# A decoder layer on one core: the down projection of the second feed-forward's last group as seven products of halves, factor columns by VectorE, and a new order

## The chip, the cores and the metric

The kernel runs on one core of one Trainium2 chip. The metric is the device time of one execution in microseconds; the time given for a kernel is the median of its runs. TensorE (PE in the profile; PEld is its loading of weights), VectorE (DVE), ScalarE (ACT), GpSimd (POOL) and the DMA queue of SyncE (SP) work side by side and wait for each other by semaphores. Each engine runs its own instructions strictly in the order in which the program holds them, so an instruction that waits holds up all that stand behind it on its engine.

## The reference

One layer of a decoder with 512 tokens and a width of 1024, all in float32. The two feed-forward parts are the ones that the change touches; `d_ff` is 2816, which is 22 tiles of 128.

```python
x = x + 1/2 * SwiGLU_1(rms(x))
h = rms(x) @ W_in                     # sparse attention (8 heads), stick-breaking attention (8 heads)
x = x + concat_heads(A, B) @ W_out
x = x + CrossAttn(rms(x), rms(mem))   # 4 heads, 256 memory tokens
x = x + 1/2 * SwiGLU_2(rms(x))

def swiglu(h, wg, wu, wd):
    return (jax.nn.silu(h @ wg) * (h @ wu)) @ wd
```

## The kernel before, in words

**Layout.** Everything is held transposed: a tile has 128 features on the partitions and the 512 tokens as columns. The stream `x` is 8 such tiles (`t_81` to `t_88` in the program's names). To keep float32 precision, each operand of a product is split into a high and a low part: ACT rounds it to the high part, DVE subtracts (`wsplit` for weights, `split` for activations). A product of two split operands is three matmuls: high by high, high by low, low by high (`mm3`, or `prod` for the halves).

**Feed-forward.** A tile of the hidden layer needs a gate and an up product over 8 tiles of the input. `ffn_up` does that plainly: 48 matmuls of 512 columns. `wino_up` (line 938) does the two together as a 2 by 2 block product with seven instead of eight products (Winograd's form of Strassen's scheme): the blocks are gate and up weights by the two halves of the inner dimension, times left and right halves of the tokens. Each of its seven products covers 4 tiles of the inner dimension, 256 columns, 3 matmuls: 84 matmuls of 256 columns, or, where the string `WIDE` marks a bank as wide, some of them as one matmul of 512 columns for two. DVE adds weights up before and sums of products behind. `right` makes the sums of the input's blocks.

The down projection is done in three groups of hidden tiles (`GROUPS`; 8, 7 and 7 in the second feed-forward). `ffn_down` (line 995) takes one group and one of the 8 output tiles: it loads the weights, splits them, runs 3 matmuls of 512 columns for each hidden tile of the group into one PSUM bank, and DVE adds the bank to `x` with a factor of -0.5. In the last group this finishes the output tile, which is then stored. The very last output tile is done in two halves of 256 columns in the same bank.

**Banks.** PSUM has 8 banks: 2 with the tag "mm", 5 "at", 1 "sm" (`BANKS`). A bank is taken again only when its last reader is done.

**Factor columns.** `rcol` (line 1135) turns a row factor `r` (the reciprocal root mean square, equal on all partitions, tokens as columns) into a column with the tokens on partitions, times -0.5. It does so with one fp32 matmul of one column for each 128 tokens: `r` as weights, a constant column `one` as operand. It is called once with 4 pieces (for the layer's attention part) and once with 2 (memory).

**Order.** All operations are recorded first, in the order of `FIRST`, `FEED` and `MIDDLE`, strings that list pieces of work (in `FEED`, "5" is the up projection of hidden tile 5, "1.3" the down projection of group 1 for output 3, "ws:0" a weight that is split early and kept in DRAM). The planner (`add_any` at line 271, `attempt` at line 342) then walks through a model of the engines: every operation has a priority, which is its place in the recording with some fixed offsets, and each engine takes the one with the lowest priority among those that are ready and whose tiles fit. All instructions are issued from one line (529 before, 656 in the changed kernel), so the profile names all of them by that line, and tiles by kind: `p` PSUM, `w` split weights or weight sums, `raw` loaded weights, `t` activations, `half` half-width sums, `d` kept weights in DRAM, `cr` and `c` constants, `s` small columns.

**The place in the middle** of which the prediction speaks: `nsa_values` (line 1607) computes the values and gates of the sparse attention for four blocks of tokens, in two "mm" and two "at" banks, 280 columns each. `v_evac` (line 1151) reads 256 of those columns with ACT and DVE, and the remaining 24 go to `gates`. `wout_sb` (line 1623), the first part of the output projection, takes an "mm" bank next. Around the same time `key_rotate` splits the rotated keys, the DVE differences of 64 rows by 512.

## Time and profile before

| | |
|---|---|
| runs, us | 1055.39, 1054.36, 1054.22; median 1054.36 |
| the profiled execution, us | 1056.67 |
| its span, first to last instruction, us | 1054.9 |
| mean granted clock of TensorE | 0.995 |
| instructions | 18656 |
| busy: PE, DVE, ACT, POOL, us | 1043.8, 923.3, 655.5, 50.8 |
| matmuls with weights of `w` or `t` and these on the right: 512 and 256 columns | 2091, 3090 |
| HBM read, written, MB | 136.93, 22.02 |

Rows of groups have the count of instructions, the busy time, the mean of one, and the idle time of the engine in front of them with what ended it. Rows of the timeline have the start, the length, the engine, the operation, the tiles and shapes, and in brackets how long the engine stood idle before and what it then followed. A row with x and a number covers so many instructions that follow each other. Busy times of instructions that overlap are counted once.

### The profile page before, as it was taken

How to read it: one execution, taken by the hardware profiler on the slowest of the kernel's cores; microseconds unless marked ns; L12 is line 12 of the kernel's file. 1: busy time of each engine (PE TensorE's matmuls, PEld its weight loads, DVE VectorE, ACT ScalarE, POOL GpSimd, SP SyncE). 2: the span in 40 equal slices, each digit the busy share in tenths (PEclk: the TensorE clock that was granted, in tenths of full speed). 3: DMA queues.
4: the chain of work that ended last, by engine and by line, in shares of the span. 5: the costliest groups of instructions: out<-in, count | busy, mean ns of one | idle time of the engine just before them, and what ended most of it. 6: DMA issues, size and time to landing. Idle time of an engine off the chain costs nothing.

```text
span 1054.9 us, 18656 instructions
## 1 busy us (share of the span) xinstructions
PE 1043.8 (99%) x6391; PEld 932.6 (88%) x6391; DVE 923.3 (88%) x1991; ACT 655.5 (62%) x1396; POOL 50.8 (5%) x93
## 2 busy tenths in 40 slices
PE   9999999999999999999999999999999999999998
PEld 8889999899888889888887888999999999898887
DVE  8999999878778869999899998899999999996842
ACT  7655656545565669899867796887665445442420
POOL 0000000000000000000003342110000000000000
PEclk9999999999999999999989999999999999999999
DMA  8174535767387732622426342654543434443421
GB/s 285 42 260 147 171 105 197 251 212 220 113 282 249 238 120 72 198 101 88 123 83 209 121 143 77 211 180 150 161 131 122 149 121 149 130 138 103 131 89 50
DMA packets 92590, 161.48 MB, mean 153 GB/s; under 512 B 11216, under 2 KB 18000, under 8 KB 92496
## 3 DMA queue, kind: packets, MB, share of 16 engines
q1 hardware_dynamic: 92064, 160.02, 47.3%
q8 instruction: 50, 0.82, 0.3%
q14 instruction: 44, 0.36, 0.1%
q10 hardware_dynamic: 432, 0.29, 0.1%
HBM read 136.93 MB, written 22.02 MB: 151 GB/s over the span
## 4 chain that ended last, share of the span: by engine, by line
PE 86%; DVE 11%; ACT 1%; issue 1%; DMA 1%; SPq 0%; DVEq 0%; ACTq 0%
PE p L529 86%; DVE t L529 7%; DVE w L529 2%; DMA t<-t 1%; ACT t L529 1%; DVE s L529 1%; ACT w L529 0%; DVE raw L529 0%; DVE gates L529 0%; SPq L529 0%; DVEq L529 0%; ACTq L529 0%; DVE one L529 0%
## 5 line engine op out<-in xcount | busy, mean ns | idle before, releaser
L529 PE MATMUL p<-t,w 128*128 128x256 f32 (+1 forms) x5181 | 887.6, 329 | 2.5 <-issue 1.5
L529 PEld LDWEIGHTS p<-t,w 128*128 128x128 f32 x5181 | 765.3, 190 | 90.2 <-DVE t L529 2.7
L529 ACT ACTIVATE w<-raw 128x512 fp32r<-128x512 f32 (+1 forms) x448 | 263.8, 613 | 191.6 <-PE p L529 113.9
L529 DVE TENSOR_TENSOR w<-raw,w 128x512 fp32r<-128x512 f32 (+1 forms) x448 | 293.0, 672 | 59.4 <-PE p L529 26.1
L529 ACT ACTIVATE t<-t 128x512 f32<-128x512 f32 (+9 forms) x463 | 220.2, 510 | 70.4 <-DVE t L529 65.8
L529 DVE TENSOR_TENSOR t<-t,t 128x512 fp32r<-128x512 f32 (+8 forms) x372 | 194.0, 543 | 9.4 <-ACT t L529 7.5
L529 DVE TENSOR_TENSOR t<-p,t 128x256 f32<-128x256 f32 (+4 forms) x194 | 96.4, 516 | 7.8 <-ACT t L529 5.6
L529 DVE SCALAR_TENSOR_TENSOR t<-p,t 128x512 f32<-128x512 f32 (+4 forms) x117 | 73.0, 632 | 30.2 <-PE p L529 28.8
L529 PE MATMUL p<-t,t 128*128 128x256 f32 (+4 forms) x450 | 96.6, 334 | 2.5 <-DVE t L529 1.1
L529 ACT ACTIVATE t<-p 128x256 f32<-128x256 f32 (+5 forms) x157 | 75.9, 502 | 28.1 <-PE p L529 25.8
L529 PEld LDWEIGHTS p<-t,t 128*128 128x128 f32 x450 | 70.7, 191 | 12.1 <-DVE t L529 2.1
L529 PE MATMUL p<-w,t 128*128 128x256 f32 (+2 forms) x304 | 53.4, 334 | 0.5 <-PE p L529 0.5
L529 DVE TENSOR_TENSOR raw<-raw,raw 128x512 f32<-128x512 f32 x76 | 52.2, 687 | 0.6
L529 PEld LDWEIGHTS p<-w,t 128*128 128x128 f32 x304 | 47.7, 202 | 5.2 <-PE p L529 0.9
L529 POOL TENSOR_SCALAR t<-t,s 128x256 f32<-128x256 f32 (+3 forms) x80 | 45.5, 588 | 105.7 <-DVE s L529 78.1
L529 DVE TENSOR_TENSOR t<-p,half 128x256 f32<-128x256 f32 x114 | 44.6, 418 | 2.0 <-PE p L529 1.8
L529 ACT ACTIVATE w<-w 128x512 fp32r<-128x512 f32 x38 | 23.8, 627 | 26.7 <-DVE w L529 21.6
L529 PE MATMUL p<-cr,t 128*128 128x128 f32 (+2 forms) x256 | 39.7, 265 | 0.0
L529 ACT ACTIVATE t<-t,g 128x256 fp32r<-128x256 f32 (+1 forms) x40 | 23.5, 588 | 21.4 <-DVE t L529 19.2
L529 PEld LDWEIGHTS p<-cr,t 128*128 128x128 f32 x256 | 32.0, 152 | 4.2 <-ACT t L529 0.5
L529 PE MATMUL p<-t,cr 128*128 128x512 f32 (+4 forms) x114 | 30.9, 329 | 1.3 <-DVE t L529 1.3
L529 POOL CAST t<-t 64x512 fp32r<-64x512 f32 (+2 forms) x9 | 5.1, 571 | 553.4 <-ACT t L529 471.4
(79 smaller groups left out, 437.9 us busy)
## 6 DMA issues: line engine op xcount, KB each, us to landing
raw<-in_ws_dram SPq DMA_DIRECT2D x362, 256.0 KB, 3.0
w<-d SPq DMA_DIRECT2D x108, 256.0 KB, 3.4
d<-w SPq DMA_DIRECT2D x76, 256.0 KB, 4.2
raw<-in_wraw_dram SPq DMA_DIRECT2D x16, 256.0 KB, 4.0
raw<-in_ws_dram SPq DMA_DIRECT2D x16, 192.0 KB, 2.6
t<-in_xT_dram SPq DMA_DIRECT2D x8, 256.0 KB, 4.4
raw<-in_ws_dram SPq DMA_DIRECT2D x14, 128.0 KB, 3.2
out_dram<-t SPq DMA_DIRECT2D x7, 256.0 KB, 2.0
```

What stands on the lines that cost most here:

```text
L529: return getattr(getattr(self.nc, op.eng), method)(*args, **kw)
```

## The change

It has these parts.

1. The second feed-forward's groups are 7, 7 and 8 hidden tiles. The last group's down projection is done for two output tiles at a time by `seven_down`: a 2 by 2 block product with seven products, of weights (two outputs by two halves of the hidden tiles) and activations (two halves of the hidden tiles by left and right token halves). `mixed` makes the sums of the activations' blocks, for each pair of hidden tiles that stand 4 apart. Of the first four hidden tiles only the left half is split as such. `wino_up` hands back its unsplit result for this.
2. `rcol` multiplies `r` by the identity on DVE and sums over the columns, in one instruction for each 128 tokens, instead of the matmul.
3. Every tile's number, counted as they are made, can have an offset (`SHIFT`), which is added to the priority of the operations recorded while it is the newest. The strings `FIRST`, `WIDE`, `FEED` and `MIDDLE` are new. In `FIRST`, 7 hidden tiles instead of 6 of the first feed-forward are done by `ffn_up`.
4. `ffn_down` takes a bank for each half of its output where it works in halves; that case was the last output of group 2, which `seven_down` now does.

```diff
-FIRST = "a0 up b0 up a2 up b2 a1 b1 a3 up b3 up up"
+FIRST = "a2 up up a0 up a1 up b0 a3 b2 b1 up b3 up up"
-GROUPS = {"1": (6, 8, 8), "2": (8, 7, 7)}
-WIDE = {"1": "z-x-x-xx-xxzxx---xz-xz", "2": "------x-----zz--zzzz--"}
+GROUPS = {"1": (6, 8, 8), "2": (7, 7, 8)}
+SEVEN = {"1": "", "2": "2"}
+WIDE = {"1": "z-z-xzxx-xxxxz-x-xzxzx", "2": "------x-----zz--zzzz--"}
...
+        "2": """0 2 4 5 1 3 6 0.2 0.5 8 0.6 7 13 19 10 0.1 0.0 0.3 12 11 0.7 9 1.3 14 18 1.4 0.4 15 1.0 16 17 1.2 1.5 1.1 20 1.6 21
+1.7 2.2 2.4 2.0 2.6"""}
+SHIFT = """2:-3 3:-3 4:-3 15:-3 16:3 21:120 22:40 24:-150 27:300 36:150 37:150 39:-3 40:-3 41:-3 42:-20 43:-20 44:-20 45:-20
...
-        op.prio = op.idx + self.bias
+        op.seg = self.seg
+        op.prio = op.idx + self.bias + self.shift.get(self.seg, 0)
...
-        self.split(ut, a[0], a[1])
+        c = slice(0, H if half else T)
+        self.split(ut[:, c], a[0][:, c], a[1][:, c])
+        return ut
+    def mixed(self, first, second, u1, u2, D, i):
...
+        minus(t12[:, L], u1[:, L], u1[:, R])
+        negative(t12[:, R], t12[:, L], u2[:, R])
+        minus(t34[:, L], u2[:, R], u1[:, R])
+        negative(t34[:, R], t12[:, R], u2[:, L])
+        D["b11", i] = tuple(x[:, L] for x in first)
+        D["b21", i] = tuple(x[:, L] for x in second)
+        D["b22", i] = tuple(x[:, R] for x in second)
+        for names, t in ((("t1", "t2"), t12), (("t3", "t4"), t34)):
+            parts = self.pair()
+            self.split(t, *parts)
...
+    def seven_down(self, k, c, j, D, done, halves):
...
+        X, Q, V = self.ps("mm")[:, :H], self.ps("at")[:, :H], self.ps("at")
...
+        prod(X, self.wsplit(a11), "b11")
+        nc.scalar.activation(g[:, R], X, AF.Copy)
+        prod(Q, self.wsplit(a12), "b21")
+        nc.vector.tensor_tensor(g[:, L], Q, g[:, R], OP.add)
+        s1 = add(a21, a22, self.wtile("w", F32, NW))
+        prod(V[:, L], self.wsplit(a22), "t4")
+        s3 = add(a11, a21, a21)
+        s2 = add(s1, a11, a11)
+        prod(X, self.wsplit(s2), "t2", first=False)
+        nc.scalar.activation(u2, X, AF.Copy)
+        prod(V[:, R], self.wsplit(s1), "t1")
+        prod(X, self.wsplit(s3), "t3", first=False)
+        nc.scalar.activation(u3, X, AF.Copy)
+        onto(x2, V, 0.5)
+        both = "p (a n) -> p a n"
+        onto(x2.rearrange(both, a=2), u3[:, None, :].to_broadcast([P, 2, H]), 0.5)
+        done(j + 1, slice(0, T))
+        if halves:
+            onto(x1[:, L], g[:, L])
+            done(j, L)
+        s4 = add(a12, s2, a12)
+        prod(V[:, R], self.wsplit(s4), "b22", first=False)
+        if halves:
+            onto(x1[:, R], u2)
+            onto(x1[:, R], V[:, R])
+            done(j, R)
+        else:
+            nc.vector.tensor_tensor(g[:, R], V[:, R], u2, OP.add)
+            onto(x1, g)
+            done(j, slice(0, T))
...
     def rcol(self, r, n):
         nc = self.nc
-        ps = self.ps("sm")
-        for t in range(n):
-            nc.tensor.matmul(ps[:, t:t + 1], r[:, t * P:(t + 1) * P], self.one, start=(t == 0), stop=(t == n - 1),
-                             skip_group_check=True)
         out = self.small([P, NT], tag="rcol", bufs=2)
-        nc.vector.tensor_copy(out[:, :n], ps[:, :n])
+        t = self.t2()
+        for i in range(n):
+            s = slice(i * P, (i + 1) * P)
+            nc.vector.tensor_tensor_reduce(t[:, s], r[:, s], self.cf[:, R_ID:R_ID + P], -0.5, 0.0, OP.mult, OP.add,
+                                           accum_out=out[:, i:i + 1])
         return out
```

In the built program there are now 1980 matmuls of 512 columns and 3276 of 256 of the kind of the table, against 2091 and 3090.

## The prediction

> **What bounds the kernel now.** I read the page's busy table first, then the waits of TensorE, then the time cut into stretches.

> ```profile
> PE 1043.8 (99%) x6391; PEld 932.6 (88%) x6391; DVE 923.3 (88%) x1991; ACT 655.5 (62%) x1396; POOL 50.8 (5%) x93
> ```

> TensorE (PE) is busy for 1043.8 of 1054.9 us. Since overlapping matmuls make that share look better than it is, its waits decide:

> ```profile
> PE p L529 <- DVE t L529: 4.1, 5, 1.3
> PE p L529 <- issue: 1.5, 1, 1.5
> PE p L529 <- DMA t<-t: 1.0, 1, 1.0
> ```

> It waited about 7 us altogether, and the last stretch has next to none of it. The stretches show where VectorE (DVE) has room, in columns of length, busy time of PE, PEld, DVE, ACT and POOL, granted clock and DMA:

> ```profile
> 400.00:500.00 100.00, 100.00 (x572) 87.99 (x572) 93.26 (x213) 92.03 (x203) 2.74 (x4) 1.00 0.37 119
> 530.00:540.00 10.00, 8.28 (x42) 7.67 (x42) 9.94 (x21) 7.93 (x20) 0.00 (x0) 0.66 0.13 38
> 550.00:560.00 10.00, 8.54 (x48) 7.45 (x48) 9.30 (x27) 6.87 (x16) 1.83 (x3) 0.83 0.95 277
> 800.00:900.00 100.00, 100.00 (x703) 93.23 (x702) 99.08 (x193) 50.01 (x86) 0.00 (x0) 1.00 0.45 140
> 900.00:950.00 50.00, 50.00 (x312) 44.80 (x311) 46.12 (x89) 23.32 (x40) 0.00 (x0) 1.00 0.43 131
> 1000.00:1046.00 46.00, 46.00 (x206) 37.96 (x205) 16.99 (x29) 9.27 (x16) 0.00 (x0) 1.00 0.23 75
> ```

> So time follows TensorE's instructions almost everywhere. In 800 to 900 us VectorE is full as well (99.08 of 100) and TensorE still never waits: the two can run level. Only the last 46 us, the down projections that change, leave VectorE 29 us of room. The middle loses both to waits and to a granted clock of 0.66 and 0.83.

> **Price of a matmul.** In the last stage every 21 matmuls of 512 columns end in one read by VectorE:

> ```profile
> 1036.36 0.69 DVE L529 SCALAR_TENSOR_TENSOR t<-p,t 128x512 f32<-128x512 f32 x1 [1.65 <-PE p L529]
> 1041.12 0.69 DVE L529 SCALAR_TENSOR_TENSOR t<-p,t 128x512 f32<-128x512 f32 x1 [4.07 <-PE p L529]
> 1045.88 0.69 DVE L529 SCALAR_TENSOR_TENSOR t<-p,t 128x512 f32<-128x512 f32 x1 [4.07 <-PE p L529]
> ```

> They stand 4.76 us apart: 0.2267 us for a wide matmul. From 200 to 300 us TensorE ran without a gap on two forms:

> ```profile
> L529 PE MATMUL p<-t,w 128*128 128x512 f32 x249 | 61.9, 391 | 0.0
> L529 PE MATMUL p<-t,w 128*128 128x256 f32 x358 | 49.3, 283 | 0.0
> ```

> (100 - 249 x 0.2267) / 358 = 0.1217 us for a narrow one; 800 to 900 us (136 wide, 567 narrow) gives 0.122. I use 0.1218. Two narrow ones thus cost 0.017 more than a wide one: halving products has a price.

> **Down projections.** Group 2 had 8, 7 and 7 tiles: 507 wide and 42 narrow matmuls. Now the first two groups take 336 wide, and the last four pairs 7 products x 4 tiles x 3 = 84 narrow each, 336. That is -171 x 0.2267 + 294 x 0.1218 = -38.77 + 35.81 = -2.96 us.

> **First feed-forward.** A seventh tile is done plainly (48 wide matmuls instead of a seven-product one), and the string of wide banks changes: together +60 wide, -108 narrow = +13.60 - 13.15 = +0.45 us. Both together: **-2.5 us**, all of it on TensorE's path. [...]

> **Factor columns.** Six fp32 products with one column go; each is two passes:

> ```profile
> 368.00 0.95 PE L529 MATMUL p<-one,t 128*128 128x1 f32 x8
> 368.81 1.42 PE L529 MATMUL p<-w,t 128*128 128x512 f32 x5
> 408.15 0.50 PE L529 MATMUL p<-one,t 128*128 128x1 f32 x4
> 408.51 0.36 PE L529 MATMUL p<-t,cr 128*128 128x256 f32 x1
> ```

> From start to the next start: 0.81 + 0.36 = **-1.2 us** of TensorE. VectorE gets six multiply-and-reduce over 128 columns in place of two small copies. Their nearest rows:

> ```profile
> L529 DVE CUSTOM_DVE_ANT_0 t<-p,t 128x512 f32<-128x512 f32 x16 | 10.5, 682 | 0.0
> L529 DVE CUSTOM_DVE_ANT_0 t<-p,t 128x384 f32<-128x384 f32 x16 | 8.5, 549 | 0.3 <-PE p L529 0.3
> L529 DVE DVE_READ_ACCUMULATOR2_ANT s<- 128x1 f32 x32 | 2.6, 82 | 0.0
> ```

> The slope (133 ns per 128 columns) gives 283 + 82 ns, 2.2 us for six. At 400 to 500 us VectorE has 6.7 us free and TensorE does not wait: nothing, or 1.9 us if that room is gone.

> **The end.** The last output was done in two halves of one bank, and the second waited for the read of the first:

> ```profile
> 1048.39 0.42 DVE L529 SCALAR_TENSOR_TENSOR t<-p,t 128x256 f32<-128x256 f32 x1 [1.82 <-PE p L529]
> 1048.87 2.77 PE L529 MATMUL p<-t,w 128*128 128x256 f32 x21 [0.52 <-DVE t L529]
> 1051.67 0.42 DVE L529 SCALAR_TENSOR_TENSOR t<-p,t 128x256 f32<-128x256 f32 x1 [2.86 <-PE p L529]
> ```

> Now the last product adds onto a bank that VectorE reads during the product before it (12 x 0.1218 = 1.46 us against a read of 0.69). The chain behind the last product is the same, one 128x256 read and one store. **-0.5 us** (the bracket of the second row).

> **The middle.** TensorE stood still before the output projection's first product, and the seven matmuls behind ran at 0.41 instead of 0.227 us:

> ```profile
> 555.90 2.87 PE L529 MATMUL p<-t,w 128*128 128x512 f32 x7 [1.46 <-issue]
> 552.26 0.42 DVE L529 TENSOR_SCALAR gates<-p,s 128x24 f32<-128x24 f32 x2
> 553.88 1.39 DVE L529 TENSOR_TENSOR t<-t,t 64x512 fp32r<-64x512 f32 x2
> 555.31 0.88 DVE L529 SCALAR_TENSOR_TENSOR t<-p,s,t 128x256 fp32r<-128x256 f32 x2
> ```

> What it waited for is the "mm" bank, which the read at 555.31 frees. On VectorE, where the combined value projection is read out, stood before (p_1750, p_1751 are its "mm" banks):

> ```order
> L529 TENSOR_SCALAR gates<-p_1750,s_1139 128x24
> L529 TENSOR_SCALAR gates<-p_1751,s_1139 128x24
> L529 TENSOR_TENSOR t_1830<-p_1829,t_1830 128x256
> L529 TENSOR_SCALAR gates<-p_1752,s_1139 128x24
> L529 TENSOR_TENSOR t_1837<-p_1836,c 128x256
> L529 TENSOR_SCALAR gates<-p_1753,s_1139 128x24
> L529 TENSOR_REDUCE s_1831<-t_1830 128x8
> L529 TENSOR_TENSOR t_1744<-t_1688,t_1743 64x512
> L529 TENSOR_TENSOR t_1746<-t_1688,t_1745 64x512
> L529 SCALAR_TENSOR_TENSOR t_1778<-p_1750,s_1139,t_1778 128x4x64
> ```

> and there stands now (p_1748 is the first "mm" bank):

> ```order
> L656 TENSOR_SCALAR gates<-p_1748,s_1174 128x24
> L656 TENSOR_TENSOR t_1969<-p_1968,t_1969 128x256
> L656 TENSOR_SCALAR gates<-p_1749,s_1174 128x24
> L656 TENSOR_REDUCE s_1970<-t_1969 128x8
> L656 TENSOR_SCALAR gates<-p_1750,s_1174 128x24
> L656 SCALAR_TENSOR_TENSOR t_1776<-p_1748,s_1174,t_1776 128x4x64
> L656 TENSOR_TENSOR t_1742<-t_1684,t_1741 64x512
> L656 TENSOR_TENSOR t_1738<-t_1668,t_1737 64x512
> ```

> The read moved ahead of the two 64x512 differences of the rotated keys (1.39 us) and of a gate and an addition. The stall and its slow stretch cost 1.46 + 7 x (0.41 - 0.227) = 2.74 us; between 0 and -2.74 I take **-2.0**, since the read now stands over 1.5 us earlier. [...] The row of 0.83 in this stretch, with no gap beyond 1.46, speaks for the higher figure.

> The other middle stall stays. It waits for the one "sm" bank through a chain of ACT and DVE steps, and the new order has the same products around it, 24 of 64 columns where 27 were:

> ```profile
> 527.61 3.09 PE L529 MATMUL p<-t,t 128*128 128x64 f32 x27
> 531.96 0.76 PE L529 MATMUL p<-t,cr 128*128 128x512 f32 x2 [1.25 <-DVE t L529]
> 533.19 8.02 PE L529 MATMUL p<-w,t 128*128 128x256 f32 x41 [0.47 <-PE p L529]
> ```

> Three fewer at 0.11 us each could lengthen it by 0.3; I count 0.

> **What VectorE gets in the last stage.** Its steps follow each other at 0.60 us for 512 columns, less than the 0.69 shown of one:

> ```profile
> 846.39 0.69 DVE L529 TENSOR_TENSOR raw<-raw,raw 128x512 f32<-128x512 f32 x1
> 846.99 0.69 DVE L529 TENSOR_TENSOR t<-t,t 128x512 fp32r<-128x512 f32 x1
> 847.59 0.69 DVE L529 TENSOR_TENSOR w<-raw,w 128x512 fp32r<-128x512 f32 x1
> 841.18 0.75 DVE L529 TENSOR_TENSOR t<-p,half 128x256 f32<-128x256 f32 x2
> 841.84 0.68 DVE L529 TENSOR_TENSOR w<-w,w 128x512 fp32r<-128x512 f32 x1
> ```

> and 0.33 for 256. A pair of outputs was two times (low part of 512, of 384, one read); it is now, for the second pair of the four (w low part, raw and w weight sums):

> ```order
> L656 TENSOR_TENSOR w_3312<-raw_3301,w_3311 128x512
> L656 TENSOR_TENSOR t_3285<-p_3281,t_3285 128x256
> L656 TENSOR_TENSOR w_3314<-raw_3302,w_3313 128x512
> L656 TENSOR_TENSOR w_3315<-raw_3303,raw_3304 128x512
> L656 TENSOR_TENSOR raw_3303<-raw_3301,raw_3303 128x512
> L656 TENSOR_TENSOR raw_3301<-w_3315,raw_3301 128x512
> L656 TENSOR_TENSOR w_3317<-raw_3304,w_3316 128x512
> L656 TENSOR_TENSOR raw_3302<-raw_3302,raw_3301 128x512
> L656 SCALAR_TENSOR_TENSOR t_84<-p_3282,t_84 128x512
> L656 TENSOR_TENSOR w_3321<-w_3315,w_3320 128x512
> ```

> Sums of one pair now stand between reads of the pair before, so a read that is late holds up the next weights. Per pair: 7 low parts, 4 sums and 3 reads of 512, 2 of 256: 14 x 0.60 + 2 x 0.33 = 9.1 us, against 84 x 0.1218 = 10.2 of TensorE. The operands (four differences of 256, two low parts of 512, less the right half that four tiles no longer split) add 2.5 us for each of four tile pairs before that. Over the whole second feed-forward VectorE has 361 steps of 512, 16 of 384 and 235 of 256 columns (326, 16, 204 before): about 303 us, against 460 wide and 1813 narrow matmuls, 325 us. It fits, as in 800 to 900 us, with little to spare at the end: from the first low part of the first pair on, 62 steps of 512 and 17 of 256, 42.9 us, stand beside 42.3 us of matmuls (336 narrow, 6 wide). TensorE has 73 older matmuls (12.6 us) ahead of that point, VectorE some 5.5 us of steps: a lead of about 7 us. I take **+0.7** for a late weight or two; bounds 0 and, with the 0.69 and 0.42 of single steps and no lead, 49.7 - 42.3 = 7.4. ACT (9 of 46 us there) and DMA (share 0.23, four more stores and loads of kept weights) have room.

> **Sum**, against the profiled execution's 1056.7 us (span 1054.9 and 1.8 around it): -2.5 - 1.2 - 0.5 - 2.0 + 0.7 = -5.5, 1051.2. The median of the runs, 1054.4, lies 2.3 lower: **1048.9 us**.

> **Rivals.**
> - *The middle gives nothing.* TensorE comes earlier to the keys that DMA copies together, where it already waited 1.0 us (the third row of the waits), and waits there instead: 1048.9 + 2.0 = 1050.9. For it speaks that those copies hang on the DMA, against it that two more output products stand before them. 0.18.
> - *The middle gives more*: the slow clock of 0.66 behind 531.96 goes too, at 41 x (0.196 - 0.122) = 3.0 us: 1045.9. The order shows no reason. 0.08.
> - *VectorE late in some pairs*: half of the 7.4 instead of 0.7, 1052. For it: reads stand between the sums. Against it: 800 to 900 us. 0.16.
> - *Slower*: the last stage becomes VectorE's. Each read waits for its product, the sums queue behind, nothing runs ahead: +7.4, and such stalls bring the half clock at 1.3 to 3 us, as at 555.90 and 533.19. 1048.2 + 7.4 + 2 = 1057.6. It decides when the lead at the first pair is gone and steps take over 0.67 us. 0.10.

> The likeliest, as summed, has 0.48; its own range is 1047 to 1050.5.

> **Chances.** 0.2% is about what a measurement here can tell from no change: below 1052.25 is faster, above 1056.47 slower. Faster: 0.48 + 0.17 + 0.08 + 0.04 = 0.77; same 0.13; slower 0.10. The range 1045.5 to 1054.5 leaves out the slower case, the late pairs' upper end and little below.

> **What would show it.** No gap of TensorE over 0.3 us before the output projection's first product near 550 us (the middle), and granted clock above 0.95 there; no product with the column "one"; TensorE without waits in the last 45 us and VectorE above 90% busy; 256-column matmuls at 0.122 each in the last pairs. Waits of TensorE for w behind VectorE in the last four pairs, or a clock below 1 there, would make the prediction wrong.

## The result and the profile after

The changed kernel takes 1045.74 us (median of 1044.51 to 1045.77), the kernel before 1054.88 beside it: a ratio of 0.991, 95% interval 0.9893 to 0.9927, 9.1 us faster. Measured again beside two of the experiments it was 10.3 us faster (0.9903, 0.9887 to 0.992). The forecast was 5.5 us, 1048.9. The direction and most of the places were right, the size was not: 1045.74 lies below the 1047 to 1050.5 of the likeliest case and at the low edge of the whole range, 1045.5 to 1054.5, and the second measurement, 1044.90, lies below that edge. In the table of experiments, one of the five runs of the changed first part took 1444.43 us at a granted clock of 0.655; its ratio leaves that run out.

The profiled execution of the changed kernel took 1045.75 us with a span of 1044.0. First the page's line of the busy times:

```profile
PE 1036.1 (99%) x6454; PEld 931.4 (89%) x6454; DVE 950.1 (91%) x2058; ACT 670.0 (64%) x1424; POOL 49.6 (5%) x92
```

Then the view of TensorE's waits (total us, times, longest):

```profile
PE p L656 <- ACT t L656: 2.2, 4, 1.1
PE p L656 <- DVE t L656: 1.9, 4, 1.1
PE p L656 <- issue: 0.3, 1, 0.3
```

TensorE's waits fell from 7.7 us (6.6 in the three rows shown of before, the rest in smaller ones) to 4.4. VectorE has 27 us more work than before and is still no bound. The stretches, in the columns used before:

```profile
400.00:500.00 100.00, 100.00 (x550) 87.23 (x549) 88.85 (x200) 88.08 (x191) 1.50 (x2) 1.00 0.36 118
530.00:540.00 10.00, 9.48 (x51) 8.48 (x52) 9.86 (x24) 7.80 (x18) 0.00 (x0) 0.69 0.13 40
550.00:560.00 10.00, 9.66 (x60) 8.10 (x58) 9.75 (x28) 6.30 (x17) 1.22 (x2) 1.00 1.01 312
800.00:900.00 100.00, 100.00 (x650) 91.41 (x650) 96.93 (x188) 47.87 (x86) 0.00 (x0) 1.00 0.42 134
1000.00:1044.00 44.00, 40.71 (x337) 40.36 (x335) 34.73 (x62) 17.58 (x35) 0.00 (x0) 1.00 0.26 85
```

At 550 to 560 us the clock is back at 1.00, at 530 to 540 it is about as low as before (0.69 against 0.66). The last stage has TensorE busy to its end (it ends at 1040.7) and VectorE at 34.73 of 44 us. The two places of the middle, from TensorE's timeline:

```profile
530.33 1.30 PE L656 MATMUL p<-t,cr 128*128 128x512 f32 x2 [1.08 <-ACT t L656]
531.82 6.81 PE L656 MATMUL p<-w,t 128*128 128x256 f32 x37 [0.19 <-DVE t L656]
...
552.03 2.29 PE L656 MATMUL p<-t,w 128*128 128x512 f32 x9 [0.34 <-issue]
```

And TensorE's groups by form in the last stage, 1000 to 1044 us (count, busy us, mean ns):

```profile
L656 PE MATMUL p<-t,w 128*128 128x256 f32 x333 | 40.6, 283 | 0.0
L656 PE MATMUL p<-t,w 128*128 128x512 f32 x4 | 1.5, 398 | 0.0
```

The output projection's first product at 552.03 waits 0.34 us where it waited 1.46, and its nine wide matmuls take 2.29 us, at a clock of 1.00. The stall near 530 us is still there, 1.08 and 0.19 us for 1.25 and 0.47. In the last stage no wait is left, and the two last rows with the 40.71 us above give the price of a narrow matmul: (40.71 - 4 x 0.2267) / 333 = 0.1195 us. That is a little low, since the view counts matmuls that began before 1000 us too; from start to start the trace has 0.120 here, as mean and as median, and not 0.1218.

To compare kernels I use one more measure, called loss below: the time from each matmul's start to the next, less the usual start-to-start time of its form (the median over both kernels). It holds waits and half-speed stretches. How a total splits depends somewhat on how finely forms are told apart. Over the whole program the usual times fell by 3.5 us (1018.4 to 1014.9) and the loss by 7.4 (31.9 to 24.5), 5.7 of it ahead of the second feed-forward; with forms told apart by shape alone it is 4.2 and 6.7. The profiled execution of before was one of its longer ones, 1.8 us above its median, so that some 2 us of this is no gain of the change.

### The profile page after: what moved, and what is told of

Read it like the earlier page. It is cut to its first block, busy times and chain, and to the rows that moved or that the text cites. A ratio compares the mean times of both kernels' runs of the same rounds, so it can differ in the third digit from the quotient of the medians.

```text
span 1044.0 us, 18955 instructions
## 1 busy us (share of the span) xinstructions
PE 1036.1 (99%) x6454; PEld 931.4 (89%) x6454; DVE 950.1 (91%) x2058; ACT 670.0 (64%) x1424; POOL 49.6 (5%) x92
## 4 chain that ended last, share of the span: by engine, by line
PE 91%; DVE 6%; DMA 1%; ACT 1%; issue 1%; SPq 0%; DVEq 0%; ACTq 0%
PE p L656 91%; DVE t L656 4%; ACT t L656 1%; DVE s L656 1%; DMA d<-w 1%; DMA raw<-in_ws_dram 1%; DVE w L656 0%; DVE gates L656 0%; ACT w L656 0%; SPq L656 0%; DVEq L656 0%; ACTq L656 0%
## 5 line engine op out<-in xcount | busy, mean ns | idle before, releaser
L656 PE MATMUL p<-t,w 128*128 128x256 f32 (+1 forms) x5256 | 880.4, 325 | 1.2 <-ACT t L656 0.8
L656 PEld LDWEIGHTS p<-t,w 128*128 128x128 f32 x5256 | 766.6, 190 | 83.6 <-DVE t L656 2.2
L656 ACT ACTIVATE w<-raw 128x512 fp32r<-128x512 f32 (+2 forms) x454 | 267.3, 613 | 163.1 <-PE p L656 79.2
L656 DVE TENSOR_TENSOR w<-raw,w 128x512 fp32r<-128x512 f32 (+2 forms) x454 | 297.4, 671 | 39.3 <-ACT w L656 15.2
L656 ACT ACTIVATE t<-t 128x256 fp32r<-128x256 f32 (+8 forms) x471 | 224.2, 511 | 87.9 <-DVE t L656 83.3
L656 DVE TENSOR_TENSOR t<-t,t 128x512 fp32r<-128x512 f32 (+9 forms) x384 | 200.3, 541 | 8.6 <-ACT t L656 6.2
L656 DVE TENSOR_TENSOR t<-p,t 128x256 f32<-128x256 f32 (+4 forms) x198 | 98.0, 513 | 10.1 <-ACT t L656 6.1
L656 ACT ACTIVATE t<-p 128x256 f32<-128x256 f32 (+4 forms) x162 | 78.1, 502 | 39.7 <-PE p L656 37.6
L656 PE MATMUL p<-t,t 128*128 128x256 f32 (+4 forms) x450 | 97.4, 334 | 0.5 <-ACT t L656 0.3
L656 DVE SCALAR_TENSOR_TENSOR t<-p,t 128x512 f32<-128x512 f32 (+3 forms) x115 | 71.7, 633 | 15.1 <-PE p L656 10.4
L656 PEld LDWEIGHTS p<-t,t 128*128 128x128 f32 x450 | 70.4, 189 | 10.3 <-ACT t L656 2.2
L656 DVE TENSOR_TENSOR raw<-raw,raw 128x512 f32<-128x512 f32 x82 | 56.2, 686 | 0.5
L656 PE MATMUL p<-w,t 128*128 128x256 f32 (+2 forms) x304 | 52.4, 329 | 0.2 <-DVE t L656 0.2
L656 PEld LDWEIGHTS p<-w,t 128*128 128x128 f32 x304 | 46.9, 197 | 4.8 <-PE p L656 0.7
L656 POOL TENSOR_SCALAR t<-t,s 128x256 f32<-128x256 f32 (+3 forms) x80 | 43.9, 568 | 105.6 <-DVE s L656 92.9
L656 DVE TENSOR_TENSOR t<-p,half 128x256 f32<-128x256 f32 x114 | 45.0, 418 | 1.7 <-PE p L656 1.2
L656 ACT ACTIVATE w<-w 128x512 fp32r<-128x512 f32 x41 | 25.6, 625 | 26.1 <-DVE w L656 15.2
L656 PE MATMUL p<-cr,t 128*128 128x128 f32 (+2 forms) x256 | 39.2, 264 | 0.3 <-DVE t L656 0.3
L656 PEld LDWEIGHTS p<-cr,t 128*128 128x128 f32 x256 | 31.8, 151 | 3.9 <-DVE t L656 0.5
L656 POOL CAST t<-t 64x512 fp32r<-64x512 f32 (+1 forms) x8 | 5.5, 691 | 549.2 <-DVE t L656 328.5
L656 PE MATMUL p<-t,cr 128*128 128x512 f32 (+4 forms) x114 | 30.5, 332 | 1.1 <-ACT t L656 1.1
L656 ACT ACTIVATE half<-p 128x256 f32<-128x256 f32 x44 | 16.5, 376 | 20.1 <-PE p L656 19.9
```

Source lines behind the costliest of these rows:

```text
L656: return getattr(getattr(self.nc, op.eng), method)(*args, **kw)
```

## The experiments

The runs stood beside the kernel before: median, and ratio to it with its 95% interval.

| run | us | ratio |
|---|---|---|
| seven products alone | 1050.81 | 0.9963 (0.995 to 0.9975) |
| own bank for each half of the last output | 1053.34 | 0.9989 (0.998 to 0.9997) |
| early read of the value projection alone | 1061.58 | 1.0067 (1.0055 to 1.008) |
| factor columns alone | 1059.59 | 1.0047 (1.0033 to 1.006) |
| changed first part alone | 1050.66 | 0.9961 (0.9947 to 0.9974) |
| changed, factor columns back on TensorE | 1072.26 | 1.0157 (1.0139 to 1.0174) |
| changed, without offsets | 1047.17 | 0.9928 (0.9914 to 0.9941) |
| the same again | 1046.69 | 0.992 (0.9905 to 0.9935) |
| changed, beside the row above | 1044.90 | 0.9903 (0.9887 to 0.992) |
| changed, 8 more VectorE steps in the last stage | 1046.37 | 0.992 (0.9905 to 0.9935) |
| changed, 16 more | 1047.92 | 0.9935 (0.9922 to 0.9947) |
| changed, other bank near 530 us | 1044.60 | 0.9911 (0.9896 to 0.9926) |
| the same again | 1045.15 | 0.991 (0.9895 to 0.9925) |
| changed, thin products added | 1072.74 | one run |

**The seven products alone.** The kernel before with part 1 of the change and the order of its second feed-forward, nothing else:

```diff
-GROUPS = {"1": (6, 8, 8), "2": (8, 7, 7)}
+GROUPS = {"1": (6, 8, 8), "2": (7, 7, 8)}
+SEVEN = {"1": "", "2": "2"}
```

> The kernel before with the last group's seven products of halves alone (groups of 7, 7 and 8 tiles and their order in the second feed-forward; first part, middle and factor columns as before, no offsets). Two sizes are told apart. By the forecast: -171 x 0.2267 + 294 x 0.1218 = -3.0, +0.7 for weights that come late from VectorE, -0.5 at the end: 2.8 us faster, with waits of TensorE for weights in the last 45 us. By start-to-start times of the changed kernel's trace (0.120 us per narrow matmul) and no late weights: -3.5 - 0.6 = 4.1 us faster, no waits there. Rival on the other side: VectorE decides the last stage, up to 6 us slower.

It was 4.0 us faster (2.6 to 5.3). Two stretches of its profile:

```profile
550.00:560.00 10.00, 8.37 (x48) 7.31 (x47) 9.46 (x27) 6.87 (x17) 1.83 (x3) 0.83 0.97 297
1000.00:1046.00 46.00, 46.00 (x367) 45.08 (x365) 39.85 (x72) 20.65 (x41) 0.00 (x0) 1.00 0.26 84
```

The middle is as before, stall and slow clock included, so the gain is the second feed-forward's own. The last 46 us are full and without a wait. The sum of the forms' usual times fell by 3.5 us, and the wait of 0.52 us at the end went. The size of the forecast (2.8) lies inside the interval too, so the median alone does not decide between the two; the missing waits do.

**A bank of its own for each half of the last output**, part 4 of the change by itself:

```diff
-        ps = self.ps("mm" if j % 2 else "at")
...
+            ps = self.ps("mm" if (i + j) % 2 else "at")
```

> The kernel before with a bank of its own for each half of the last output. The forecast's term: the wait of 0.52 us between the two halves goes and nothing comes in its place: 0.5 us faster, no half-speed stretch left or made. Rival: the last read and the store decide the end, and TensorE's earlier finish is worth nothing: 0.

It was 1.2 us faster (0.3 to 2.1), and the wait between the halves is gone from TensorE's timeline, whose last row runs to the end without one:

```profile
1041.69 7.00 PE L529 MATMUL p<-t,w 128*128 128x512 f32 x50
```

So 0.5 is confirmed within what this can tell. The profile taught something else. Its order up to the last output is that of the kernel before, so the stall before the output projection is there, but not what followed it. TensorE's timeline, then the stretch:

```profile
554.16 0.30 PE L529 MATMUL p<-t,s 128*32 128x64 f32 x2
556.08 1.86 PE L529 MATMUL p<-t,w 128*128 128x512 f32 x7 [1.63 <-issue]
```

```profile
550.00:560.00 10.00, 8.37 (x59) 7.24 (x58) 9.84 (x29) 7.07 (x17) 1.83 (x3) 1.00 0.94 289
```

The same seven matmuls behind a stall of 1.63 us took 1.86 us, at a clock of 1.00; in the profile of before they took 2.87 behind one of 1.46. The slow stretch does not belong to the stall as such (more on it in the last section).

**The early read alone.** In the kernel before, the reads of the value projection's banks get an earlier priority:

```diff
+            nc.bias -= 300
             self.v_evac(ps[:, :256], col[:, t:t + 1], v)
+            nc.bias += 300
```

> The kernel before with the reads of the combined value projection alone put ahead of the two 64x512 key differences on VectorE. Theory A: the stall of 1.46 us before the output projection is that bank's, and the slow stretch behind it is the stall's: both go, 2.3 to 2.8 us faster, granted clock at 550 to 560 us back from 0.83 to 1.00. Theory B (the slow clock needs a longer idle time and is not the stall's doing): the stall goes, 1.1 to 1.5 us faster, clock there still 0.83. Theory C (the middle gives nothing): TensorE stands still a little later at the keys copied by DMA, 0 to 0.5 us faster.

At the place itself theory A came true, and the kernel still became 6.8 us slower. Three stretches of its profile, then two rows of TensorE's timeline:

```profile
550.00:560.00 10.00, 9.96 (x63) 8.18 (x63) 9.63 (x27) 7.03 (x17) 1.83 (x3) 1.00 0.92 284
560.00:570.00 10.00, 8.41 (x48) 6.59 (x48) 9.98 (x36) 5.33 (x22) 3.66 (x8) 1.00 0.88 271
690.00:700.00 10.00, 8.33 (x54) 7.70 (x53) 10.00 (x30) 8.95 (x25) 0.00 (x0) 0.84 0.72 237
```

```profile
567.48 0.44 PE L529 MATMUL p<-cr,t 128*128 128x128 f32 x2 [1.13 <-DVE t L529]
...
695.90 2.33 PE L529 MATMUL p<-t,w 128*128 128x256 f32 x8 [1.61 <-ACT t L529]
```

From 550 to 560 us TensorE is busy for 9.96 us at full clock: the bank was what the product waited for. But the planner puts everything behind the moved read in new places. TensorE then waits 1.13 us at 567.48 and 1.61 at 695.90, the latter ahead of eight matmuls of 256 columns that take 2.33 us, at a clock of 0.84 in the third row; the loss at 680 to 720 us rose from 2.0 to 6.3, at 600 to 660 from 5.4 to 8.1.

**The factor columns alone** (part 2, the new `rcol` in the kernel before):

> The kernel before with the factor columns alone moved from TensorE to VectorE. The forecast's term: six fp32 one-column products go, 0.81 + 0.36 us of TensorE, and VectorE's six multiply-and-reduce steps (about 2.2 us) lie in its free time: 1.2 us faster, waits elsewhere as before within 0.5. Rival: those products stood where TensorE would have waited anyway, or VectorE's steps come late there: 0 to +1 us.

The matmuls' usual times fell by 1.1 us, as forecast, yet the kernel was 4.8 slower: the loss rose by 3.9 even against the long profile of before. The largest piece, from the timeline:

```profile
693.69 0.58 PE L529 MATMUL p<-cr,t 128*128 128x2 f32 x4 [0.48 <-ACT t L529]
694.13 0.71 PE L529 MATMUL p<-t,t 128*128 128x256 f32 x4
695.81 0.50 PE L529 MATMUL p<-t,w 128*128 128x256 f32 x2 [0.96 <-ACT t L529]
696.76 5.05 PE L529 MATMUL p<-t,w 128*128 128x256 f32 x24 [0.45 <-DVE t L529]
```

This is the memory attention, some 290 us behind the last of the moved columns. Neither theory had that: the cost of the edit is not where the edit is. How the moved columns lead to waits so much later is not shown.

**The changed kernel with the factor columns back on TensorE**, the same edit from the other side:

> The changed kernel with the factor columns back on TensorE, all else as changed; the planner places everything behind that point anew. The forecast's term alone: 1.2 us slower than the changed kernel (about 1047). After the same edit by itself in the kernel before took 1.1 us of matmuls away and yet lost 4.8 by waits further on: if a plan that was fitted to its products loses some 3 us with any edit in the middle, 3 to 6 us slower than the changed kernel (1049 to 1052).

It was 27 us slower than the changed kernel, far beyond both sizes expected. The largest of its stalls:

```profile
424.19 0.92 PE L656 MATMUL p<-w,t 128*128 128x256 f32 x6
428.26 7.93 PE L656 MATMUL p<-t,w 128*128 128x512 f32 x22 [3.15 <-DVE t L656]
```

A wait of 3.15 us and 22 wide matmuls at some 0.36 us. The matmuls' usual times rose by only 0.7. So the strings and offsets of the change belong to its operations: with this one put back, they are worth less than none.

**The changed first part alone**: the change's strings up to the second feed-forward and its factor columns, with the second feed-forward of before and no offsets:

> The changed kernel's first part alone (its tables up to the second feed-forward, and the factor columns on VectorE), with the second feed-forward of the kernel before and no offsets. If the parts add up, the changed kernel without offsets (7.9 us faster than before) less the seven products (4.0) leaves 3.9 us faster than before, of which 0.5 are matmuls (0.66 for the first feed-forward's wider mix against 1.13 for the factor columns) and the rest shorter waits between 500 and 720 us. By the forecast's terms (+0.45 - 1.2 - 2.0): 2.75 faster. If the middle's gain belongs to the offsets or hangs on the second part's order: 0 to 1 us faster.

It was 4.3 us faster (2.7 to 5.6), which agrees with 3.9 and, just, with the forecast's 2.75. The place of the stall of 1.46 us, and the ten us behind it:

```profile
550.00:560.00 10.00, 9.70 (x59) 8.44 (x59) 9.91 (x29) 6.30 (x17) 0.84 (x2) 1.00 1.00 319
560.00:570.00 10.00, 8.88 (x54) 6.97 (x54) 10.00 (x37) 9.63 (x40) 4.02 (x9) 1.00 0.71 241
```

The stall is gone without the offsets. In the ten us behind, where VectorE is full, TensorE waits twice, the second time at 565.56; the run with the own bank, which has the order of before, shows no such wait there:

```profile
560.92 0.30 PE L534 MATMUL p<-t,s 128*32 128x64 f32 x2 [0.34 <-DVE t L534]
565.56 0.62 PE L534 MATMUL p<-t,t 128*128 128x256 f32 x3 [0.78 <-ACT t L534]
```

```profile
560.00:570.00 10.00, 9.88 (x59) 8.29 (x58) 9.96 (x35) 7.80 (x32) 3.41 (x8) 1.00 0.94 300
```

The profile of before itself has 9.01 there, with a wait of 0.97 us for a DMA that the two other profiles of its order lack. With the offsets the wait of 0.78 us is one of 0.32. Since each kernel's loss varies with the execution, I took means over the profiles that share a first part. Loss in us, with a row for each stretch:

| stretch, us | order of before (3 profiles) | of the change, no offsets (3) | with offsets (6) |
|---|---|---|---|
| 0 to 200 | 3.1 | 3.2 | 2.6 |
| 200 to 515 | 5.1 | 3.8 | 4.2 |
| 515 to 545 | 5.3 | 4.6 | 4.8 |
| 545 to 570 | 4.3 | 3.1 | 2.8 |
| 570 to 720 | 9.6 | 9.2 | 8.5 |

So the new order takes about 2 us out of 515 to 570, and about 1 out of 200 to 515, where the first feed-forward ends and the products of the attention begin. With the offsets the five rows together fall by another 1.0, of which 0.3 is at 545 to 570 and 0.7 behind it.

**Without the offsets**, in two runs, the second beside the changed kernel:

```diff
-SHIFT = """2:-3 3:-3 4:-3 15:-3 16:3 21:120 ...
+SHIFT = ""
```

> The changed kernel without the offsets per tile, tables and products as changed. If the offsets only fine-tune: 0 to 2 us slower than the changed kernel, the waits of the middle as there. If they are what keeps the middle's waits short (forecast: the middle is worth 2.0 us, 2.7 by the trace of the change): 3 to 8 us slower, with all of the loss in waits and half-clock windows between 500 and 720 us, and none in the last 45 us.

> The changed kernel without the offsets, beside the changed kernel. If the offsets are a term of their own that the forecast left out: 1.4 us slower than the changed kernel, and with the seven products (4.0) and the first part (4.3) they make up the 9.1. If those two parts are all of it: within 0.5 us of the changed kernel, and the earlier 1.4 was the difference between chips and phases of the clock.

> The changed kernel itself, for the two below to be measured against on the same chip: 9.1 us faster than before, as measured, within 0.7.

Beside each other, 1046.69 (1045.52 to 1047.15) stands against 1044.90 (1044.35 to 1045.29): the offsets are worth 1.8 us, a term of its own (1.4 by the first run, 1047.17 against 1045.74). They are a fine-tuning, not what holds the middle together: without them 600 to 680 us reads, first row, and with them, second row (two kernels):

```profile
600.00:680.00 80.00, 78.69 (x570) 72.72 (x569) 71.89 (x207) 65.92 (x168) 21.41 (x32) 1.00 0.46 142
```

```profile
600.00:680.00 80.00, 79.71 (x576) 73.48 (x575) 71.13 (x206) 66.00 (x168) 21.09 (x32) 1.00 0.47 145
```

TensorE works for one us more in the same time; where the rest lies is not shown. With this the parts add up: the seven products and the first part, measured apart, give 4.0 + 4.3 = 8.3, against 7.9 and 8.5 measured together without the offsets, and with the offsets 10.1, against 9.1 and 10.3.

**More VectorE work in the last stage**, which the forecast's slower rival and its allowance of 0.7 us were about:

```diff
         s1 = add(a21, a22, self.wtile("w", F32, NW))
+        for _ in range(2):
+            add(a21, a22, s1)
```

> The changed kernel with two repeats of one 512-column weight sum in each of the last four pairs (8 more VectorE steps, 4.8 us at 0.60). If VectorE has the room that the trace of the change shows in the last 44 us (9.3 us free): within 0.5 us of the changed kernel, no TensorE wait there. By the forecast's slower rival, the last stage becomes VectorE's once its steps take 5 us more: 2 to 7 us slower.

> The changed kernel with four repeats of the same weight sum in each of the last four pairs (16 more VectorE steps, 9.6 us at 0.60). VectorE then has about as much work as there is time in the last stage: 1 to 3 us slower, with TensorE waits for VectorE's weights in the last pairs. If it stays within 0.5 us, the allowance of 0.7 us for late weights had no ground at all; if it is over 5 us slower, the stage stood at the edge.

The last stage with two repeats a pair (4.8 us), then with four (9.6 us), then TensorE's timeline with four:

```profile
1000.00:1044.00 44.00, 42.12 (x343) 41.47 (x341) 39.91 (x71) 18.11 (x37) 0.00 (x0) 1.00 0.26 91
```

```profile
1000.00:1044.00 44.00, 41.26 (x331) 39.99 (x329) 41.97 (x75) 17.95 (x37) 0.00 (x0) 1.00 0.27 89
```

```profile
1029.51 1.45 PE L656 MATMUL p<-t,w 128*128 128x256 f32 x10 [0.44 <-DVE w L656]
1031.43 8.83 PE L656 MATMUL p<-t,w 128*128 128x256 f32 x70 [0.47 <-ACT half L656]
1040.56 1.95 PE L656 MATMUL p<-t,w 128*128 128x256 f32 x12 [0.31 <-DVE t L656]
```

The first has no wait in the last stage and a loss of 0.4 us there. Its median is 0.6 and 1.5 us above the changed kernel's two, more than the 0.5 expected, but the rest of its loss lies ahead of 720 us, where every engine's order is that of the changed kernel, and so is not the stage's. The second has waits for weights and halves and a loss of 2.8; its median is 2.2 to 3.0 us above the changed kernel's two. So the stage turns into VectorE's between 5 and 10 us of added work, and the change itself stands clear of that.

**Another bank near 530 us.** The forecast had said that the stall there waits for the one "sm" bank. Every engine's order stays as it is:

```diff
-        self.head_norm(t, gcol, d)
+        self.head_norm(t, gcol, d, "mm" if gcol == G_KW else "sm")
```

> The changed kernel with the second rotated key's sum of squares in a bank of the mm kind in place of the single sm bank; every engine's order is the same. If, as the forecast had it, the stall near 530 us waits for that bank: the stall of 1.08 us goes or shrinks to a third, and the half-clock windows behind it may go too, 1 to 4 us faster than the changed kernel. If it is the chain of ACT and VectorE steps that make the product's operands: the same time, the stall within 0.3 us of 1.08.

> The changed kernel with the second rotated key's sum of squares in an mm bank, beside the changed kernel. The earlier profile had the stall split in three (0.48, 0.60, 0.49 us) in place of 1.08 and 0.19. If that is worth nothing: within 0.5 us of the changed kernel. If the earlier median holds: 1.1 us faster.

TensorE's timeline in the second run:

```profile
529.34 0.69 PE L656 MATMUL p<-t,cr 128*128 128x512 f32 x1 [0.47 <-ACT t L656]
530.46 0.80 PE L656 MATMUL p<-t,cr 128*128 128x512 f32 x1 [0.42 <-DVE t L656]
531.45 5.79 PE L656 MATMUL p<-w,t 128*128 128x256 f32 x27 [0.19 <-DVE t L656]
```

The first of the two products starts 0.6 us earlier, so it had waited for the bank; the second then waits 0.42 for its low part from VectorE, and the next group starts when it did (531.45 here, 531.47 in the changed kernel's profile beside it). The time is the same, 1045.15 against 1044.90. The first run's 1044.60, which looked faster, was not. Both theories held half of it: the first product waited for the bank, but what ends the wait last is VectorE's chain. None of the variants is faster than the changed kernel beyond what these runs can tell.

**Thin products.** To see what lowers the clock without any wait, 64 extra matmuls stand ahead of the first product of three of the last pairs:

```diff
+        n = {0: 64, 2: 128, 4: 80}.get(j, 0)
+        for _ in range(64 if n else 0):
+            nc.tensor.matmul(X[:, :n], D["b11", 0][0][:, :P], D["b11", 0][0][:, :n], start=True, stop=True)
```

> The changed kernel with 64 extra matmuls of 128, 80 and 64 columns ahead of the first product of three of the last four pairs (their sums are overwritten; nothing else is left out). They follow each other at about 0.11 us, so TensorE is never idle in them, while a window of 3.41 us streams about 4,000, 2,500 and 2,000 columns. If the granted clock goes by the columns streamed in the window before (about 3,000, as the traces so far have it): no half-clock window behind the 128-column block, one or two behind each of the others. If it goes by idle time: none behind any. All in all 20 to 26 us slower.

It was 27 to 28 us slower than the changed kernel, a little more than expected, and behind the 64-column block the half clock lasted from 1038.2 to about 1048.4 us, three windows of 3.41 us, not one or two. TensorE's timeline with the 128-column and the 64-column block, then stretches around the second:

```profile
1000.74 6.36 PE L656 MATMUL p<-t 128*128 128x128 f32 x56
1006.94 8.84 PE L656 MATMUL p<-t,w 128*128 128x256 f32 x72
...
1035.49 5.66 PE L656 MATMUL p<-t 128*128 128x64 f32 x38
```

```profile
1034.00:1038.00 4.00, 4.00 (x39) 4.00 (x37) 3.01 (x5) 1.54 (x3) 0.00 (x0) 1.00 0.19 70
1038.00:1048.00 10.00, 10.00 (x50) 10.00 (x50) 0.69 (x1) 0.63 (x1) 0.00 (x0) 0.51 0.07 26
```

Behind the 128-column block 72 matmuls of 256 columns took 8.84 us, 0.12 each from start to start. In the 64-column block the clock fell to half at 1038.2 us, with TensorE busy all the time ahead of it and 2,592 columns streamed in the 3.41 us before: in this one execution it fell without idleness, behind few columns. Many of the 80-column products were set among products of 256 columns by the planner, and the longest row of them fell across two windows, so that no window there fell below 3,879 columns, and they tell nothing of their own.

## Why the prediction was right, and where it was not

The step that failed is the sum: of the new order it counted only the few places read in the two orders, and it put the rest, the offsets above all, at nothing without a reason. It also charged 0.7 us for late weights that did not come. The runs show 1.8 us for the offsets where the forecast had no term, 4.3 for the changed first part where it had 2.75, and 4.0 for the seven products where it had 2.8 (with the end).

- **Down projections, -2.96.** Right in kind, short in size: the narrow matmul was taken at 0.1218 us, a mean over stretches that hold small losses; in the stage itself it is 0.120, which is also the median from start to start at 200 to 300 us of before. The sum becomes -171 x 0.2267 + 294 x 0.120 = -3.5.
- **Late weights or VectorE, +0.7.** This failed. There is no wait in the last stage, and 4.8 us of VectorE work can be added for a loss of 0.4 there. The lead of some 7 us that the prediction worked out ("a lead of about 7 us") told more than the bound of 7.4 from single steps; VectorE was to be over 90% busy there and is at 79%.
- **The end, -0.5.** Right: the wait of 0.52 us is gone. With the two terms above, -4.0 where -2.8 stood; measured alone, -4.0.
- **First feed-forward, +0.45.** Not run alone. With 0.120 the same counts give 13.60 - 12.96 = +0.6.
- **Factor columns, -1.2.** Right for TensorE (1.1 measured). "Nothing" for the rest holds only in an order that was made with them; in the kernel before they cost 4.8 us.
- **The middle, -2.0.** The stall of 1.46 us went to 0.34 and the clock to 1.00, by the read that the two orders showed. The means by stretch give 1.2 us at 545 to 570, the place that the term meant (1.5 with the offsets), and 0.5 to 0.7 at 515 to 545, which it counted as 0; that the two make about 2 is partly luck. Also, the step "the stall and its slow stretch cost 2.74" took what the clock did in one execution for a fixed cost: 1.28 of it came in some of the executions only (the clock at 550 to 560 us is 0.83 in the profiles of before and of the seven products, and 1.00 in that of the own bank). And the read alone, without the rest of the new order, made the kernel slower, which no step of the prediction allowed for.
- **The stall near 530 us stays.** Right, though a little shorter; its cause was half right.
- **What had no term.** The sum had entries only for places read in the two orders. The offsets, 1.8 us, and about 1 us less loss at 200 to 515 us had none. These, the 0.7 and the narrow matmul's price make up the difference between 5.5 and the 9.1 to 10.3 measured. By which steps the loss at 200 to 515 us fell stays open.
- **The rivals.** The middle that "gives nothing" came in small part: without the offsets TensorE waits 0.78 us at 565.56, but for ACT by the profile and not for the keys' DMA, and the loss at 545 to 570 is still 1.2 lower. The one that has the slow clock at 532 us go too did not come. VectorE late in some pairs did not come either. The slower one, the last stage as VectorE's, has its turn only beyond 5 us of added work.

## What to carry to other kernels

Where a planner sets the order from priorities, an edit in the middle need not show its own price: one moved read and six moved products cost 7 and 5 us by waits as much as 290 us later, until the order was made anew, so a part is to be priced together with its order, and a term for the order itself belongs into the sum. Take the price of an instruction from the densest stretch of its form, and look at more than one execution before a slow stretch is counted as a cost. Whether a second engine bounds a stage is quickly measured by repeating one of its steps: VectorE, busy for 34.73 of the last 44 us and with a lead estimated at 7 us, was no bound here, and became one between 4.8 and 9.6 us of added work.

## What the runs showed of the hardware

The windows did not stand at the same place of the program in each execution: the first one at full clock began between 3.98 and 7.26 us in these profiles (6.88 in that of before, 7.10 in that of the changed kernel), so one and the same stall can fall into them differently. In the profile of before the stall of 1.46 us left its window with 2,684 columns; with the bank's edit a stall of 1.63 us fell almost wholly into one that was otherwise full of wide products, 4,162 columns in all, and no slow stretch followed. For the seven matmuls behind the stall that is 1.86 us against 2.87. The kernel before, in 40 runs beside these experiments, had a mean of 1055.6 us where the mean clock was 0.995 (7 runs) and 1053.9 where it was 0.998 (5 runs).
